# Reordering the Fourier steps, layer-norm work and one buffer switch of a hand-ordered stage in an encoder kernel

## The chip, the cores and the metric

The kernel runs on one core of one Trainium2 chip. The metric is device time in microseconds (us) of one execution. Engine names are those of the profile: PE is TensorE's matmuls and PEld its weight loads, DVE is VectorE, ACT ScalarE, POOL GpSimd, SP SyncE, which here only issues DMAs.

## The reference

Two sequences (2048 and 4096 tokens, 1024 channels, fp32) pass through one encoder layer:

```
h = rms_norm(x, pre_g)
a_u, a_v, a_gate, b_in, b_gate, c_in, c_gate = split(h @ w_in)        # widths 384 x5, 256 x2
ya = (gelu(a_u) * (w_s @ layer_norm(gelu(a_v)) + b_s)) * silu(a_gate) # 4 heads x 96, chunks of 128 tokens
yb = (pooled_mean(b_in) - b_in) @ w_b * scale * silu(b_gate)          # windows 2, 4, 8, 16
yc = real(fft2(c_in)) @ c_w * silu(c_gate)                            # over positions and 64 channels
y  = x + rms_norm(concat(ya, yb, yc) @ w_out, post_g)
```

The three parts are called the mixing branch (ya), the pool branch (yb) and the Fourier branch (yc) here.

## The kernel before, in words

The program has three stages. The first (0 to 483.7 us of the trace) computes the norm statistics, the inputs of the Fourier branch and its gates, and v (`a_v`), and leaves all of that and the operands of the later products in DRAM. The third (from 1389.1 us) is the output projection. Neither is touched.

The second stage is ordered by hand: every engine does its instructions in the order in which the program writes them. It computes the remaining wide projections by a scheme with seven products instead of eight, P1, P2, X1, X2, X3, Y1, Y2, each from a fp32 operand of 1024 tokens that is split into a high part (a cast on ACT, L137) and a low part (a subtraction on DVE, L138); a product of split parts is three matmuls (`mm3`, L141 to L143). The list `todo` holds 84 products, called **slots** here and counted from 0: six blocks of the pool branch (slots 0 to 41, in the order P1 X1 P2 X2 Y1 X3 Y2), then six of the mixing branch (slots 42 to 83, P1 X1 P2 X2 X3 Y1 Y2). Each slot has three groups of 12 matmuls, one for each third of the 384 output channels. `slot()` writes, in this order: the loads of the operand two slots on, the stores that wait (`stores`), weight loads, the last eviction of the slot before (`tail`), the cut of the next slot's operand, group 1, `fill_a`, its eviction, a Fourier step, group 2, weight cuts, `fill_b`, its eviction, a Fourier step, group 3, and `then` (the 128x128 mixing products). P1, X1, X2 and X3 add up in the same three PSUM banks (`Ab`, tag A in the figures below: `Aa_0` to `Aa_2`); P1 is copied out by ACT before X1 of the next slot goes on in its bank.

All loads and stores are issued by SP, in order, on one queue.

**Fourier steps.** `steps` is the list of the Fourier branch's work, and each call of `beside()` advances it by one: call n issues the store of step n-4, the load of step n, the compute part of step n-2 and the `pre` part of step n. A step may be empty. The list has

- ten **folds** (`fold_steps`): VectorE differences and sums of a sequence's halves, `fo` and `fz` (L948, L950, L138), loaded from `zz_d` and stored to `o_d`. Each fold is four steps: load, a **copy step**, compute with store, empty. The seven real copy steps (`copy_step`) are three DRAM-to-DRAM copies of weights each, that the mixing block's and the output's weight loads read;
- six **table steps** between the second and the third fold, of which two compute (tables `ttab`, `cmix`);
- for both sequences and both channel pairs a **transform** (`transform_steps`): levels 4096 (the long sequence only), 2048, 1024, whose steps load a matrix `mt` (L1018) and half an `o` (L1015) and add products `pd` in a PSUM bank of the two of tag G; the level's last step (`finish`) evicts it (`ev`, L1044, `eg`, L1045) into the row `T`. Then two base steps (`base_step`: products `pbc`, `pbs`, evictions `bm` and `T`), an empty step, and mixing steps (`mix_steps`: `pmx`, and `pny` for the last position).

Fourier tiles of one shape class share seven buffers (`ftile`, L278).

**The switch of buffers.** Pool branch and mixing branch use the same SBUF space (`e1`). Slot 42 is therefore written apart (the end of the listing): its three groups of matmuls, then all pool work that is left (`means`, `sums`, `silu`, `gate`, `close_sequence`), the stores, the closing of the pool's buffers and the opening of the mixing branch's, and only then the evictions of P1 (`ua`, L1474) and two Fourier steps.

**The mixing block.** `load_v` loads v of a half block (four chunks), `stats` computes its layer-norm statistics (DVE, L1409, L1410, and POOL), `normalise` applies them (16 ACT activations `vn`, L1423), `mix` multiplies by `w_s` (PE), `mixed`, `gelu`, `silu` and `gate` do the rest. `normalise(0)` stands in `fill_a` of the third slot of a block, `normalise(1)` in `fill_a` of the fifth.

Of the kernel before, what the change touches and what calls it, by code (L numbers as in the profile page):

```python
# [10 lines left out]
F32 = mybir.dt.float32  # L11
# [4 lines left out]
P = 128  # L16
# [17 lines left out]
def hybrid_encoder(  # L34
# [849 lines left out]
    def table_steps():  # L884
# [38 lines left out]
        return [Step(), Step(), Step(compute, load), Step(compute_mix, load_mix), Step(), Step()]  # L923
# [3 lines left out]
    def fold_steps(s, L, r):  # L927
# [40 lines left out]
        return [Step(load), copies.pop(0), Step(compute, store=store), Step()]  # L968
# [12 lines left out]
    copies += [Step(), Step(), Step()]  # L981
    T_of = {}

    def transform_steps(s, pair):
        S = SEQS[s]
        out = []

        def open_t():
            T_of[(s, pair)] = fpool.tile([P, SEQS[0] // 2 + 1], F32, tag="T", name=f"T{s}_{pair}")

        L = S
        while L >= 1024:
            out.extend(level_steps(s, L, pair, open_t if L == S else None))
            L //= 2
        for which in range(2):
            out.append(base_step(s, pair, which))
        out.append(Step())
        for kb in range(S // 2 // TB):
            out.extend(mix_steps(s, pair, kb))
        return out  # L1000

    def level_steps(s, L, pair, open_t):
# [64 lines left out]
        out.append(Step(finish))  # L1067
# [88 lines left out]
    steps[8:8] = table_steps()  # L1156
# [13 lines left out]
    def slot(j, pairs, evict, fill_a=(), fill_b=(), loads=(), then=None, cuts=(), late=False):  # L1170
# [41 lines left out]
    edge = e1.tile([P, 216], F32, name="edge")  # L1212
    corr_sb = e1.tile([P, 48], F32, name="corr_sb")
# [4 lines left out]
    def pool_means(z, n, t, name, corr_at=None):  # L1218
# [3 lines left out]
        a = e1.tile([P, TB + 16], F32, tag="a", name=f"pa{name}", bufs=6)  # L1222
        b = e1.tile([P, TB + 16], F32, tag="w", name=f"pb{name}", bufs=2)
# [5 lines left out]
        else:  # L1229
# [4 lines left out]
            else:  # L1234
                c = e1.tile([P, TB + 16], F32, tag="w", name=f"pc{name}", bufs=2)
# [110 lines left out]
    for b in range(NB // 2):  # L1346
# [18 lines left out]
        for i, m in enumerate(WIDE["b"]):  # L1365
# [7 lines left out]
            slot(7 * b + i, pairs, lambda t, ps, m=m, blk=blk: blk.evict(m, t, ps), fa[i], fb[i], loads, None, cuts, 3)  # L1373
# [3 lines left out]
    class MixBlock:  # L1377
# [6 lines left out]
        def new(self, tag, h):  # L1384
            (self.u if tag == "u" else self.ga)[h] = [
                e1.tile([P, TB], F32, tag=f"{tag}{h}", name=f"{tag}a{self.b}_{h}_{t}", bufs=3) for t in range(3)
            ]

# [26 lines left out]
        def normalise(self, h):  # L1415

            st, mv, va, rv, nb = self.ln[h]
            nc.vector.scalar_tensor_tensor(nb, mv[:, :, 0], -1.0, rv, ALU.mult, ALU.mult)  # L1418
            for c in range(NCH):
# [51 lines left out]
        def evict(self, m, t, ps):  # L1471
            u, ga = self.u, self.ga
            if m == "P1":
                nc.scalar.copy(u[1][t], ps)  # L1474
            elif m == "X1":
                nc.scalar.copy(ga[0][t], ps)
            elif m == "P2":
                nc.vector.tensor_add(u[0][t], ps, u[1][t])
# [90 lines left out]
    for b in range(NB // 2):  # L1569
# [7 lines left out]
        fb = {i: [] for i in range(7)}
        fb[6].append(lambda: blk.gate(1))
        ld = {i: [] for i in range(7)}
        ct = {i: [] for i in range(7)}  # L1580
        then = {3: lambda: blk.mix(0), 5: lambda: blk.mix(1)}
        fa[2].append(lambda: blk.normalise(0))
        fa[3].append(lambda: blk.stats(1, range(2)))
        fb[3].append(lambda: blk.stats(1, range(2, 4)))
        fa[4].append(lambda: blk.normalise(1))
        if b == 0:
            ld[1].append(lambda: blk.load_v(1))
            fb[1].append(lambda: blk.stats(0, range(4)))
            ct[0].append(lambda: cut_wide_weights("X3"))
            ld[0].append(lambda: load_wide_weights("a", "Y2"))  # L1590
            ct[1].append(lambda: cut_wide_weights("Y2"))
        else:
            fa[0] += [lambda p=prev: p.silu(0)]
# [14 lines left out]
        for i, m in enumerate(WIDE["a"]):  # L1608
            ev = lambda t, ps, m=m, blk=blk: blk.evict(m, t, ps)
            j = 7 * (b + NB // 2) + i  # L1610
            if b == 0 and i == 0:
                load_operand(j + 2)
                flush(stores)
                flush(tail)
                cut_operand(j + 1)
                op = cut.pop(j)
                pss = [pr.product(m, op) for pr in pairs]
                for f in (*ld[0], *ct[0]):
                    f()
                prev.means(1, 1)  # L1620
                prev.sums(1, 2)
                prev.silu(0)
                prev.means(1, 2)
                prev.gate(0)
                prev.gate(1)
                prev.close_sequence()
                flush(stores)
                last_pool.close()
                e1 = last_pool.enter_context(tc.tile_pool(name="e1c", bufs=1, reuse_waits="tile"))
                blk.new("u", 1)  # L1630
                blk.load_v(0)
                for t, ps in enumerate(pss):
                    ev(t, ps)
                beside()
                beside()
                continue
            slot(j, pairs, ev, fa[i], fb[i], ld[i], then.get(i), ct[i])
# [261 lines left out]
```

## Time and profile before

| | us |
|---|---|
| median of 3 runs (lowest to highest) | 1869.28 (1869.02 to 1870.66) |
| the profiled execution, its own time | 1875.17 |
| its span, first to last instruction | 1873.4 |
| first stage, 0 to 483.73 | 483.73 |
| second stage, 483.73 to 1389.13 | 905.40 |
| third stage, 1389.13 to 1873.40 | 484.27 |
| PE busy over the span | 1745.1 (93%) |
| DVE, ACT, POOL busy | 1383.5 (74%), 916.6 (49%), 429.4 (23%) |

The profile comes from one execution, whose span is its first to its last instruction; the time of that execution is a little longer. The granted clock is that of TensorE as a share of its full speed; over the span it was 0.970. "Busy" leaves out issuing of DMAs, branches and semaphores. A wait is put down to the instruction that released it last.

### The profile page before, as it was taken

To read this page: it belongs to the slowest core of one execution; us is meant where nothing else is said; L and a number is where in the kernel's file an instruction comes from. 1 tells how busy PE (TensorE), PEld (TensorE's weight loads), DVE (VectorE), ACT (ScalarE), POOL (GpSimd) and SP (SyncE) were. 2 spreads that over 40 slices of the span, in tenths; PEclk is the share of its full clock that TensorE was granted. 3 is DMA by queue.
4 is the path that set the end of the run, shared out by engine and by line. 5 is a ranking of instruction groups with operands and counts; after the bars stand their busy time and mean duration, and the time that the engine had idled before them with its cause. 6 is when DMAs were issued, how large, how long until landed. Compare 5 with 4: busy or idle time off the path is not lost. (4 is left out here: it accounts for less than half of the span.)

```text
span 1873.4 us, 27630 instructions
## 1 busy us (share of the span) xinstructions
PE 1745.1 (93%) x9784; PEld 1501.4 (80%) x9784; DVE 1383.5 (74%) x2320; ACT 916.6 (49%) x1766; POOL 429.4 (23%) x293
## 2 busy tenths in 40 slices
PE   5999999999989889999698999889989999999998
PEld 4999999999867767877486877777767888888886
DVE  8867777897687896777755675556786777777786
ACT  4766653345555453456364554645663343333332
POOL 5001121321000000000000010000005656666664
PEclk9999999999999999999799999999999999999999
DMA  7999997787859978868776577564844545454543
GB/s 250 331 341 317 369 351 267 283 313 265 294 193 300 298 266 284 284 237 273 239 260 214 188 257 250 175 239 146 276 131 159 169 155 178 160 168 158 169 157 112
DMA packets 221787, 443.83 MB, mean 237 GB/s; under 512 B 30417, under 2 KB 112977, under 8 KB 221649
## 3 DMA queue, kind: packets, MB, share of 16 engines
q1 hardware_dynamic: 221648, 442.07, 68.8%
q8 instruction: 77, 1.26, 0.3%
q14 instruction: 62, 0.50, 0.1%
HBM read 297.81 MB, written 150.47 MB: 239 GB/s over the span
## 5 line engine op out<-in xcount | busy, mean ns | idle before, releaser
L1413 POOL TENSOR_TENSOR lnst<-lnst,mhalf 128x16 f32<-128x16 f32 x12 | 37.3, 3106 | 434.5 <-DVE lnst L1412 414.2
L1731 POOL TENSOR_TENSOR cc<-cc,xr 128x1024 f32<-128x1024 f32 x46 | 110.4, 2400 | 53.4 <-DVE cc L1730 53.4
L398 DVE SCALAR_TENSOR_TENSOR xp<-xp,g_sb,rbc 128x256 f32<-128x256 f32 x192 | 98.8, 580 | 4.7 <-ACT rbc L382 3.2
L1423 ACT ACTIVATE vn<-vn,lnst 128x96 f32<-128x96 f32 x192 | 70.2, 454 | 51.4 <-DVE lnst L1418 51.4
L1672 ACT ACTIVATE junk<-cc 128x512 f32<-128x512 f32 x72 | 45.5, 632 | 80.9 <-DVE cc L1713 45.1
L137 ACT CAST yo_X<-y 128x512 fp32r<-128x512 f32 x60 | 34.9, 620 | 89.3 <-PE Xo L143 74.4
L138 DVE TENSOR_TENSOR yo_P<-y,yo_P 128x512 fp32r<-128x512 f32 x48 | 70.1, 1460 | 7.1 <-ACT yo_P L137 6.9
L1268 POOL MEMSET zb<- 128x16 f32 x6 | 0.5, 112 | 322.0 <-ACT zb L1266 261.3
L365 ACT ACTIVATE xrow<-xrow 128x512 f32<-128x512 f32 x88 | 54.9, 627 | 21.6 <-DMA xrow<-in_x_sample 20.7
L1730 DVE SCALAR_TENSOR_TENSOR cc<-cc,orr,pgb 128x512 f32<-128x512 f32 x69 | 53.8, 807 | 15.3 <-POOL orr L1680 15.3
L353 POOL TENSOR_TENSOR rr<-ssq,mhalf 128x4 f32<-128x4 f32 (+1 forms) x13 | 17.0, 1311 | 201.7 <-DVE ssq L351 138.9
L138 DVE TENSOR_TENSOR yo_X<-y,yo_X 128x512 fp32r<-128x512 f32 x48 | 59.4, 1238 | 0.2
L141 PE MATMUL pd<-mt,o 128*128 128x256 f32 (+1 forms) x80 | 27.9, 349 | 24.1 <-ACT eg L1045 9.9
L1672 ACT ACTIVATE junk<-Po 128x512 f32<-128x512 f32 x24 | 14.4, 599 | 72.3 <-PE Po L143 72.3
L137 ACT CAST yo_P<-y 128x512 fp32r<-128x512 f32 x48 | 29.4, 615 | 40.1 <-PE Xo L143 26.1
L177 DVE TENSOR_TENSOR ys<-y,y 128x512 f32<-128x512 f32 x24 | 23.8, 996 | 32.7 <-DMA y<-yc_d 32.6
L1680 POOL TENSOR_TENSOR orr<-oms,mhalf 128x1 f32<-128x1 f32 x48 | 27.1, 565 | 83.4 <-DVE oms L1678 83.4
L1409 DVE BATCH_NORM_STATS2 lnst<-vn 128x6 f32<-128x96 f32 x192 | 44.2, 230 | 0.0
L141 PE MATMUL Ab<-b_X1h,wbX1h 128*128 128x512 f32 x72 | 31.1, 432 | 14.0 <-ACT zb L1331 13.7
L1239 ACT COPY pa<-pb 32x512 f32<-32x512 f32 (+1 forms) x24 | 14.8, 619 | 58.6 <-DVE pb L1227 36.5
L191 POOL TENSOR_TENSOR y<-y,y 128x512 f32<-128x512 f32 x23 | 32.8, 1428 | 31.2 <-DVE yo_X L138 27.4
L1410 DVE BATCH_NORM_AGGREGATE lnst<-lnst 128x2 f32<-128x6 f32 x192 | 35.0, 182 | 6.6
(740 smaller groups left out, 6750.2 us busy)
## 6 DMA issues: line engine op xcount, KB each, us to landing
op_d<-xp SPq DMA_DIRECT2D x72, 512.0 KB, 5.9
mt<-const_m SPq DMA_DIRECT2D x56, 512.0 KB, 6.5
xp<-in_xt SPq DMA_DIRECT2D x48, 512.0 KB, 6.4
out<-cc SPq DMA_DIRECT2D x46, 512.0 KB, 2.9
xr<-in_x_sample SPq DMA_DIRECT2D x32, 512.0 KB, 4.2
xrow<-in_x_sample SPq DMA_DIRECT2D x28, 512.0 KB, 5.8
o<-o_d SPq DMA_DIRECT2D x40, 256.0 KB, 5.5
vn_d<-vg SPq DMA_DIRECT2D x48, 192.0 KB, 4.2
```

The source lines that it names most:

```text
L137: last_cast[0] = nc.scalar.copy(hi, src)
L138: return (nc.gpsimd if pool_lo else nc.vector).tensor_sub(lo, src, hi.bitcast(F32))
L141: nc.tensor.matmul(ps, lh, rh, start=first, stop=False, skip_group_check=True)
L365: nc.scalar.activation(half, half, AF.Square, accum_out=ss[:, 2 * c + h : 2 * c + h + 1])
L398: nc.vector.scalar_tensor_tensor(xs[q][:, sl], xs[q][:, sl], g8_sb[:, 4 * kh + k : 4 * kh + k + 1], rbc[a], ALU.mult, ALU.mult,)
L1409: nc.vector.bn_stats(st[:, j], self.v[h][c][:, 96 * hd : 96 * hd + 96])
L1410: nc.vector.bn_aggr(mv[:, j], st[:, j])
L1413: nc.gpsimd.tensor_tensor(rv, va, mhalf, ALU.pow)
L1423: nc.scalar.activation(v_, v_, AF.Identity, bias=nb[:, j : j + 1], scale=rv[:, j : j + 1])
L1672: nc.scalar.activation(junk, src, AF.Square, accum_out=ss[:, j : j + 1])
L1730: nc.vector.scalar_tensor_tensor(cc[c][:, hs], src, rr, pgb[:, hs], ALU.mult, ALU.mult)
L1731: nc.gpsimd.tensor_add(cc[c], cc[c], xr[c])
```

## The change

- **Empty steps.** Behind the last step of each level, and behind each base step, stands an empty step (before: one behind the two base steps).
- **Folds and copies.** The seven copy steps and three table steps (one empty) come first in the list, one to a call; folds have an empty step in the copy step's place.
- **Three steps to a slot.** `slot()` takes `more`: further calls of `beside()` behind the third group. It is 1 in the slots X1, P2, Y1 and X3 of the pool blocks 3 to 5 and in the slots X2 and Y1 of each mixing block. The list now has 168 steps.
- **The switch.** Slot 42 is written by `slot()` like the rest. P1 of the first mixing block goes into three tiles `s1a` of the Fourier branch's seven buffers; the pool's last `means`, `sums`, `silu` and `gate` stand in `fill_a` and `fill_b`, and `change_buffers` (stores, closing, opening, then both `load_v`) in the new place `fill_c`, ahead of the third group. `close_sequence` moves to slot 44; its tiles come out of the Fourier buffers and out of `mpool`.
- **The mixing block.** `normalise` takes a range of chunks. Chunks 0 and 1 of half 0 are done in `fill_b` of the third slot and 2 and 3 in its `fill_c`; those of half 1 in `fill_b` of the fifth and `fill_a` of the sixth. `gelu(0)` moves from `fill_a` to `fill_b` of the fourth slot, the first block takes its own `u` tiles of half 1 in the fifth slot, and the tile `m` has one buffer instead of two.

```
@@ table_steps
-        return [Step(), Step(), Step(compute, load), Step(compute_mix, load_mix), Step(), Step()]
+        return [Step(compute, load), Step(compute_mix, load_mix), Step()]
@@ fold_steps
-        return [Step(load), copies.pop(0), Step(compute, store=store), Step()]
+        return [Step(load), Step(), Step(compute, store=store), Step()]
@@ copies
-    copies += [Step(), Step(), Step()]
@@ transform_steps
         for which in range(2):
-            out.append(base_step(s, pair, which))
-        out.append(Step())
+            out.extend([base_step(s, pair, which), Step()])
@@ level_steps
-        out.append(Step(finish))
+        out.extend([Step(finish), Step()])
@@ the list
-    steps[8:8] = table_steps()
+    steps[0:0] = [*copies, *table_steps()]
@@ slot
+        for f in fill_c:
+            f()
         last = pairs[2].product(m, op)
+        for _ in range(more):
+            beside()
         if then:
             then()
@@ pool_means
-        a = e1.tile([P, TB + 16], F32, tag="a", name=f"pa{name}", bufs=6)
-        b = e1.tile([P, TB + 16], F32, tag="w", name=f"pb{name}", bufs=2)
+        def tile_(x, tag, bufs):
+            if n < TB:
+                return ftile(f"p{x}{name}", (P, n + 16))
+            return e1.tile([P, TB + 16], F32, tag=tag, name=f"p{x}{name}", bufs=bufs)
+        a, b = tile_("a", "a", 6), tile_("b", "w", 2)
@@ the pool blocks
-            slot(7 * b + i, pairs, ..., cuts, 3)
+            slot(7 * b + i, pairs, ..., cuts, 3, (), 1 if b > 2 and i in (1, 2, 4, 5) else 0)
@@ MixBlock
-        def normalise(self, h):
+        def normalise(self, h, cs):
...
-            for c in range(NCH):
+            for c in cs:
...
-                m_ = e1.tile([P, NCH, P], F32, tag="m", name=f"m{self.b}_{h}_{t}", bufs=2)
+                m_ = e1.tile([P, NCH, P], F32, tag="m", name=f"m{self.b}_{h}_{t}")
...
             if m == "P1":
-                nc.scalar.copy(u[1][t], ps)
+                nc.scalar.copy(self.s1[t], ps)
@@ the mixing blocks
-            3: [lambda: blk.new("g", 1), lambda: blk.gelu(0)], 4: [lambda: blk.mixed(0)], 5: [],
+            3: [lambda: blk.new("g", 1), lambda: blk.stats(1, range(2))], 4: [lambda: blk.mixed(0)],
+            5: [lambda: blk.normalise(1, range(2, 4))], 6: [...],
...
-        fa[2].append(lambda: blk.normalise(0))
-        fa[3].append(lambda: blk.stats(1, range(2)))
-        fb[3].append(lambda: blk.stats(1, range(2, 4)))
-        fa[4].append(lambda: blk.normalise(1))
+        fb[2] += [lambda: blk.normalise(0, range(2))]
+        fc[2] += [lambda: blk.normalise(0, range(2, 4))]
+        fb[3] += [lambda: blk.gelu(0), lambda: blk.stats(1, range(2, 4))]
+        fb[4] += [lambda: blk.normalise(1, range(2))]
         if b == 0:
+            blk.s1 = [ftile(f"s1a_{t}", (P, TB)) for t in range(3)]
+            def change_buffers():
+                nonlocal e1
+                flush(stores)
+                last_pool.close()
+                e1 = last_pool.enter_context(tc.tile_pool(name="e1c", bufs=1, reuse_waits="tile"))
+                blk.load_v(0)
+                blk.load_v(1)
...
+            fa[0] += [lambda p=prev: p.means(1, 1), lambda p=prev: p.sums(1, 2), lambda p=prev: p.silu(0)]
+            fb[0] += [lambda p=prev: p.means(1, 2), lambda p=prev: p.gate(0), lambda p=prev: p.gate(1)]
+            fc[0] += [change_buffers]
+            fc[2] += [prev.close_sequence]
...
-            slot(j, pairs, ev, fa[i], fb[i], ld[i], then.get(i), ct[i])
+            slot(j, pairs, ev, fa[i], fb[i], ld[i], then.get(i), ct[i], False, fc[i], 1 if i in (3, 5) else 0)
```

The first place is ACT in slot 51, the third slot of the second mixing block, from the cast of X2's operand to that of X3's. `vn` are the 16 normalisations, `ev` and `eg` the evictions of a level of the Fourier transform. Before:

```order
L137 CAST a_X2h<-a_X2l 128x1024 x2
L1423 ACTIVATE vn_0_9567<-vn_0_9567,lnst_0_9822 128x96 x4
L1423 ACTIVATE vn_1_9569<-vn_1_9569,lnst_0_9822 128x96 x4
L1423 ACTIVATE vn_2_9571<-vn_2_9571,lnst_0_9822 128x96 x4
L1423 ACTIVATE vn_3_9573<-vn_3_9573,lnst_0_9822 128x96 x4
L1044 COPY ev_4096_1_9987<-pd_4096_10_9173 128x512
L1045 ACTIVATE eg_4096_1_9988<-pd_4096_10_9173,cols 128x512
L137 CAST a_X3h<-a_X3l 128x1024 x2
```

With the change:

```order
L137 CAST a_X2h<-a_X2l 128x1024 x2
L1042 COPY ev_2048_1_10019<-pd_2048_10_9841 128x256
L1043 ACTIVATE eg_2048_1_10020<-pd_2048_10_9841,cols 128x256
L1433 ACTIVATE vn_0_9593<-vn_0_9593,lnst_0_9865 128x96 x4
L1433 ACTIVATE vn_1_9595<-vn_1_9595,lnst_0_9865 128x96 x4
L1433 ACTIVATE vn_2_9597<-vn_2_9597,lnst_0_9865 128x96 x4
L1433 ACTIVATE vn_3_9599<-vn_3_9599,lnst_0_9865 128x96 x4
L137 CAST a_X3h<-a_X3l 128x1024 x2
```

The normalisations now stand behind the evictions of the Fourier step, which is another level's step than before, since the list has moved.

The second place is ACT in slot 42, from the last SiLU `gb` of the pool branch to the cut of the operand of slot 44. `pa_..l` are the tiles of `close_sequence`, `Aa` the PSUM banks of P1, `ua` its place before and `s1a` now. Before:

```order
L1283 ACTIVATE gb_0_2_8502<-gb_0_2_8502 128x512
L1285 COPY gb_1_2_8658<-gb_0_2_8502 128x8
L1239 COPY pa_0l<-pb_0l 32x8
L1239 COPY pa_1l<-pb_1l 64x8
L1239 COPY pa_2l<-pc_2l 32x8
L1474 COPY ua_1_0_9100<-Aa_0_8987 128x512
L1474 COPY ua_1_1_9101<-Aa_1_9000 128x512
L1474 COPY ua_1_2_9102<-Aa_2_9013 128x512
L137 CAST a_P2h<-a_P2l 128x1024 x2
```

With the change:

```order
L1290 ACTIVATE gb_0_2_8515<-gb_0_2_8515 128x512
L1292 COPY gb_1_2_8676<-gb_0_2_8515 128x8
L1484 COPY s1a_9016<-Aa_0_9031 128x512
L855 CAST waX3h<-waX3l 128x1536
L1484 COPY s1a_9017<-Aa_1_9067 128x512
L1484 COPY s1a_9018<-Aa_2_9121 128x512
L137 CAST a_P2h<-a_P2l 128x1024 x2
```

The copies of `close_sequence` are gone from here, one weight cut stands between the evictions, and these write tiles that the new pool does not hold.

The third place is SP from the last store of the pool branch (`yb_d`) on, in slots 42 to 44. `vn` are the loads of v, `a_X2l` is the operand of slot 45, `o` and `mt` belong to a Fourier step. Before:

```order
L1325 DMA yb_d_124<-pa_2l 128x8
L1395 DMA vn_0_9103<-vn_d 128x384
L1395 DMA vn_1_9105<-vn_d 128x384
L1395 DMA vn_2_9107<-vn_d 128x384
L1395 DMA vn_3_9109<-vn_d 128x384
L1130 DMA yc_d_125<-gm_0_20_8850 128x512
L1130 DMA yc_d_125<-gm_0_21_8852 128x512
L1015 DMA o_4096_10_9116<-o_d_4096_127 128x512
L1018 DMA mt_4096_100_9118<-const_m 128x1024
L1018 DMA mt_4096_101_9130<-const_m 128x1024
L826 DMA a_X2l<-op_d 128x1024 x2
```

With the change:

```order
L1319 DMA yb_d_124<-pa_1_2_9045 128x512
L1404 DMA vn_0_9105<-vn_d 128x384
L1404 DMA vn_1_9107<-vn_d 128x384
L1404 DMA vn_2_9109<-vn_d 128x384
L1404 DMA vn_3_9111<-vn_d 128x384
L1404 DMA vn_0_9113<-vn_d 128x384
L1404 DMA vn_1_9115<-vn_d 128x384
L1404 DMA vn_2_9117<-vn_d 128x384
L1404 DMA vn_3_9119<-vn_d 128x384
L826 DMA a_X2l<-op_d 128x1024 x2
L1013 DMA o_4096_13_9159<-o_d_4096_127 128x512
L1016 DMA mt_4096_130_9161<-const_m 128x1024
```

Eight loads of v instead of four stand behind the stores, and the operand and the next matrix now come behind these.

## Rows read from the trace of the kernel before

**Rows 1.** The page: span and instructions

```profile
span 1873.4 us, 27630 instructions
```

**Rows 2.** Busy time of the hand-ordered stage (us, engines' busy, PEclk, DMA share, GB/s)

```profile
483.73:1389.13 905.40, 825.81 (x4571) 674.36 (x4570) 632.39 (x1240) 469.96 (x848) 41.17 (x30) 0.95 0.71 241
```

**Rows 3.** The same, slots 9, 26, 64, 4-8, 25, 42-43, 51, 63-65, 71-72

```profile
573.43:581.59 8.16, 8.16 (x37) 6.76 (x36) 6.36 (x14) 3.73 (x5) 0.00 (x0) 1.00 0.70 229
...
738.02:747.54 9.52, 9.52 (x43) 7.88 (x42) 3.05 (x3) 5.61 (x13) 0.22 (x2) 1.00 0.71 249
...
1161.79:1170.70 8.91, 8.91 (x43) 7.47 (x42) 5.55 (x22) 4.24 (x7) 1.49 (x1) 1.00 0.85 276
...
516.37:573.43 57.06, 46.22 (x189) 36.17 (x188) 45.04 (x72) 29.97 (x60) 0.00 (x0) 0.91 0.65 214
...
721.27:738.02 16.75, 12.71 (x43) 9.60 (x42) 12.24 (x17) 5.30 (x8) 0.00 (x0) 0.80 0.80 278
...
894.21:936.20 41.99, 24.41 (x87) 19.25 (x86) 31.39 (x79) 13.86 (x24) 2.90 (x1) 0.76 0.68 229
...
1009.97:1028.25 18.28, 11.93 (x44) 9.38 (x43) 5.79 (x9) 9.38 (x21) 0.00 (x0) 0.81 0.40 144
...
1148.82:1186.51 37.69, 31.55 (x137) 25.96 (x136) 19.07 (x53) 19.75 (x39) 2.90 (x1) 0.91 0.62 202
...
1240.70:1270.41 29.71, 23.27 (x94) 18.92 (x92) 9.94 (x28) 12.64 (x27) 2.90 (x1) 0.83 0.50 180
```

**Rows 4.** PE's waits in that stage: who waited for whom, total us, times, longest

```profile
PE Ab L141 <- ACT zb L1331: 13.7, 3, 6.0
PE pny L1142 <- ACT ua L1474: 13.1, 1, 13.1
PE pd L141 <- ACT eg L1045: 9.9, 4, 5.6
PE pd L141 <- DMA mt<-const_m: 6.7, 3, 4.0
PE pbs L1088 <- ACT T L1060: 4.6, 1, 4.6
PE pd L141 <- DVE lnst L1409: 4.5, 1, 4.5
PE pbc L1088 <- ACT bm L1090: 3.9, 1, 3.9
```

**Rows 5.** DVE groups, 500 to 720 us: line, operation, xcount, busy us, mean ns

```profile
L948 DVE TENSOR_TENSOR fo<-fz,fz 128x132 f32<-128x132 f32 (+1 forms) x80 | 17.2, 284 | 4.1 <-DMA fz<-zz_d 4.0
...
L950 DVE TENSOR_TENSOR fz<-fz,fz 128x512 f32<-128x512 f32 x20 | 13.8, 689 | 0.3
L138 DVE TENSOR_TENSOR fo<-fo,fh 128x512 fp32r<-128x512 f32 x20 | 13.7, 685 | 1.8 <-ACT fh L137 1.8
```

**Rows 6.** Timeline of ACT in slot 51: start, duration, line, operation

```profile
1014.23 5.84 ACT L1423 ACTIVATE vn<-vn,lnst 128x96 f32<-128x96 f32 x16 [1.57 <-DVE lnst L1418]
1019.97 0.56 ACT L1044 COPY ev<-pd 128x512 f32<-128x512 f32 x1
```

**Rows 7.** Timelines of DVE, SP and ACT in slot 42

```profile
908.55 3.86 DVE L1305 TENSOR_TENSOR pa<-pa,gb 128x512 f32<-128x512 f32 x6
...
909.26 3.49 SPq L1312 DMA_DIRECT2D yb_d<-pa  x6
...
909.91 0.20 ACT L1285 COPY gb<-gb 128x8 f32<-128x8 f32 x1
...
916.40 1.56 ACT L1474 COPY ua<-Aa 128x512 f32<-128x512 f32 x3 [0.82 <-DVE pa_2l L1323]
```

**Rows 8.** DMA issues: KB of each, median us from issue to landing

```profile
mt<-const_m SPq DMA_DIRECT2D x56, 512.0 KB, 6.5
...
yb_d<-pa SPq DMA_DIRECT2D x30, 256.0 KB, 6.4
```

**Rows 9.** Busy time of the stretch in which the transfers were densest

```profile
600.00:620.00 20.00, 20.00 (x89) 16.39 (x88) 17.93 (x31) 12.63 (x27) 0.00 (x0) 1.00 1.00 328
```

More of the change, by code (lines that the diff above doesn't have):

```diff
@@ L1168, in flush, with slot @@
             f()
-    def slot(j, pairs, evict, fill_a=(), fill_b=(), loads=(), then=None, cuts=(), late=False):
+    def slot(j, pairs, evict, fill_a=(), fill_b=(), loads=(), then=None, cuts=(), late=False, fill_c=(), more=0):
         m = todo[j][2]
@@ L1372, in hybrid_encoder @@
                     cuts.append(lambda i=i: cut_wide_weights(WIDE["b"][i - 2]))
-            slot(7 * b + i, pairs, lambda t, ps, m=m, blk=blk: blk.evict(m, t, ps), fa[i], fb[i], loads, None, cuts, 3)
+            slot(7 * b + i, pairs, lambda t, ps, m=m, blk=blk: blk.evict(m, t, ps), fa[i], fb[i], loads, None, cuts, 3, (), 1 if b > 2 and i in (1, 2, 4, 5) else 0)
         before = blk
@@ L1384, in new @@
         def new(self, tag, h):
-            (self.u if tag == "u" else self.ga)[h] = [
+            (self.u if tag == "u" else self.ga)[h] = ts_ = [
                 e1.tile([P, TB], F32, tag=f"{tag}{h}", name=f"{tag}a{self.b}_{h}_{t}", bufs=3) for t in range(3)
             ]
+            if tag == "u" and h == 1 and self.b > 0:
+                self.s1 = ts_
         def load_v(self, h):
@@ L1413, in stats @@
                 nc.gpsimd.tensor_tensor(rv, va, mhalf, ALU.pow)
[L1415 removed]
+        def normalise(self, h, cs):
             st, mv, va, rv, nb = self.ln[h]
[L1418 to L1419 removed]
+            if cs[0] == 0:
+                nc.vector.scalar_tensor_tensor(nb, mv[:, :, 0], -1.0, rv, ALU.mult, ALU.mult)
+            for c in cs:
                 for hd in range(4):
@@ L1477, in evict @@
             elif m == "P2":
-                nc.vector.tensor_add(u[0][t], ps, u[1][t])
+                nc.vector.tensor_add(u[0][t], ps, self.s1[t])
             elif m == "X2":
@@ L1572, in hybrid_encoder @@
         fa = {
-            0: [lambda: blk.new("u", 1)], 1: [lambda: blk.new("g", 0)], 2: [lambda: blk.new("u", 0)],
-            3: [lambda: blk.new("g", 1), lambda: blk.gelu(0)], 4: [lambda: blk.mixed(0)], 5: [],
-            6: [lambda: blk.silu(1), lambda: blk.mixed(1)],
-        }
[L1577 to L1580, printed above, removed]
+            0: [], 1: [lambda: blk.new("g", 0)], 2: [lambda: blk.new("u", 0)],
@@ new lines, in hybrid_encoder @@
+            3: [lambda: blk.new("g", 1), lambda: blk.stats(1, range(2))], 4: [lambda: blk.mixed(0)],
+            5: [lambda: blk.normalise(1, range(2, 4))], 6: [lambda: blk.silu(1), lambda: blk.mixed(1)],
+        }
+        fb, fc, ld, ct = ({i: [] for i in range(7)} for _ in range(4))
+        fb[2] += [lambda: blk.normalise(0, range(2))]
+        fc[2] += [lambda: blk.normalise(0, range(2, 4))]
+        fb[3] += [lambda: blk.gelu(0), lambda: blk.stats(1, range(2, 4))]
+        fb[4] += [lambda: blk.normalise(1, range(2))]
@@ L1592, in hybrid_encoder @@
         else:
-            fa[0] += [lambda p=prev: p.silu(0)]
+            fa[0] += [lambda p=prev: p.silu(0), lambda: blk.new("u", 1)]
             fb[0] += [lambda p=prev: p.gate(0), lambda: blk.stats(0, range(2))]
@@ L1610, in hybrid_encoder @@
             j = 7 * (b + NB // 2) + i
[L1611 to L1636, printed above, removed]
-            slot(j, pairs, ev, fa[i], fb[i], ld[i], then.get(i), ct[i])
+            slot(j, pairs, ev, fa[i], fb[i], ld[i], then.get(i), ct[i], False, fc[i], 1 if i in (3, 5) else 0)
         prev = blk
```

17 lines of the change are left out of this document (9 added, 8 removed).

## Prediction

> **What bounds the kernel now.** I read the page first. Its span is 1873.4 us [rows 1]. The change touches only the hand-ordered stage, 905.40 of those microseconds; PE is busy for 825.81 there and the mean granted clock is 0.95 [rows 2]. So the loss is in holes on PE, and in time after some holes at the lower of its two levels (1.2 instead of 2.4 GHz). The third view cuts that stage into slots [rows 3]. An undisturbed slot of 36 products lasts 8.16 us, one with two 512-column Fourier steps 9.52, one with a 256-column step 8.91. Whatever a slot lasts beyond that is loss: 57.06 against 5 x 8.16 = 40.8 in slots 4 to 8 (16.3 lost), 41.99 against 19.0 in slots 42 and 43 (23.0), 18.28 against 8.9 in slot 51 (9.4), 37.69 against about 27.8 in slots 63 to 65 (9.9), 29.71 against about 18.8 in slots 71 and 72 (10.9). The fourth view names what ended PE's waits [rows 4]: ScalarE copies mostly, in four places. The matmuls are the same ones after the change, so only these losses can move.
>
> **Part A, fold steps and copies (slots 0 to 9).** The seven copy steps leave the folds and run alone in slots 1 to 4; the folds start ten steps later, in slots 7, 9, 11 and so on instead of 2, 4 and then 9. A fold costs VectorE 17.2/10 + 13.8/10 + 13.7/10 = 4.5 us [rows 5]. Two of them, 9 us, leave the slots in which five weight cuts also run; this backlog is what slots 4 to 8 wait for. One fold returns in slot 7, whose P1 evictions slot 8 needs; the wait of that kind was 13.7 us in three places [rows 4], so one could cost 6 with its clock. I take 3, since no fold precedes it. The 21 DRAM-to-DRAM copies keep their bytes and come where fold loads and stores were, so I cost them at nothing; if they delayed the operands, slots 3 to 5 would wait. Gain 16.3 - 3 = **13** (6 to 16). From slot 9 to 23 folds stand where they stood, and their losses stay.
>
> **Part B, the switch of buffers (slots 42 and 43).** Before, the three P1 evictions wait in ScalarE's queue for the new pool, hence for the pool branch's gating (3.86 us, done 18.2 us into the slot); the evictions start at 916.40, and PE's next step stands behind them: 13.1 us, then 4.5 more [rows 4, 7]. Now P1 goes into three Fourier buffers, so that PE goes on. But VectorE's and ScalarE's lists up to the gating are the same but for one weight cut, and the SiLUs still stand ahead of the first eviction; they ended 15.9 us into slot 42 (910.11 less 894.21 [rows 7]). VectorE has some 2 us less to do just before, so I put the first copy's end at 13; X1's first product, due at 9.5, waits 3.5. The gating ends no earlier than the 18.2 of now, so the six yb stores still leave SP at 15 to 18 us or later (3.49 us for all [rows 7]). Behind them SP now holds eight loads of v, then X2's operand, then the matrix of the step that PE reaches first in slot 44: gating done at 20, eight loads about 4.5 (some 0.5 us an issue, as the stores show), operand and o 1.5, landing 6.5 for mt [rows 8], together 32.5. PE would want it at 9.5 + 3.5 + 9.5 + 2.7 = 25.2, and waits some 7.5; issues here also wait for older transfers, so I say 8.5. For the clock after two holes I put 5: the stretch of slots 42 and 43 ran at 0.76, 10 us of 41.99 [rows 3], about half of them inside the holes themselves. After: 3.5 + 8.5 + 5 = 17. Gain 23 - 17 = **6** (-2 if the statistics on VectorE hold up slot 45 too; 18 if the matrix comes in time).
>
> **Part C, Fourier steps in the mixing blocks (slots 44 to 75).** In slot 51 ScalarE first does 16 normalisations, 5.84 us, and only then the eviction `ev` that frees the accumulator for the next level [rows 6]; PE waits 5.6 of the 9.9 us of that kind [rows 4]. Now those 16 stand behind the second and third product, after the step's own work, and an empty step separates a level's eviction from the next level's first product, and one base step from the next. The waits on `eg`, on `T` and on `bm` (9.9 + 4.6 + 3.9 [rows 4]) are of that sort. Slots 51, 63 to 65, 71 and 72 lose 9.4 + 9.9 + 10.9 = 30.2; of this I leave 3.5 to a matrix that landed late. To it come some 6 us in single waits elsewhere (the rest of `eg`, the ny steps). Gain 26.7 + 6 = **33** (20, if one wait in three returns in another place, to 40). The vector work per slot does not grow, and the single `m` buffer costs nothing, since one engine writes and reads it.
>
> **Part D, three steps to a slot.** From slot 22 on four of seven pool slots carry three steps. A matrix buffer is freed one step before the load is issued and wanted three steps later: 1.5 slots before, now one slot of about 10.2 us less the step itself, against a landing of 6.5 [rows 8]. That holds with 2 to 3 us to spare. Traffic in such a slot is 2 x 512 KB of operand, 3 x 512 KB of matrix, 1.5 x 256 KB of o and some stores, 3.2 MB in 10.2 us or 318 GB/s; the densest stretch of the trace shows 328 GB/s at a DMA share of 1.00 [rows 9]. So transfers will run close to full, and the first step of the transform, which stands behind ten fold stores on SP, still waits. I take **-6** for waits on matrices and tables, late vector work (P1 to X1 at the start of blocks) and their clock, between -1 (none of weight) and -14 (two waits of 4 us with clock).
>
> The Trainium skill, "DMA: Bandwidth & Descriptors", section Specifications, puts the limit of HBM for one core at about 358 GB/s. By that figure a three-step slot would leave a tenth of the bandwidth free, part D would be about -2 and the time 1819. The trace does not bear it out: its share is full at 328 GB/s, so I keep -6.
>
> **Sum.** 13 + 6 + 33 - 6 = 46 us. The profiled execution took 1875.17 us, 1.8 more than its span and 5.9 more than the median of the three runs, so it would become 1829; against the median 1869.28 - 46 = **1823**. The ends are 6 - 2 + 20 - 14 = 10 and 16 + 18 + 40 - 1 = 73, that is 1859 and 1796.
>
> **Rivals.** (1) Slower: DMA cannot feed three steps to a slot. Ten three-step slots follow the start of the transform up to slot 41. If the matrix is late in each by what the first one is late now (4.0 us at the longest [rows 4]) and the clock falls each time (3.4 us, 0.20 of slot 25's 16.75 [rows 3]), 74 us go against the 52 of the other parts: 1891. It decides from about eight late slots. For it: 318 against 328 GB/s, one queue in order. Against: a late load delays the loads behind it no further, and level 4096 covers only six of these slots. (2) SP's queue at the switch is worse than I say: v loads, operand and matrix come after both the stores' landing (6.4 [rows 8]) and VectorE's statistics, and slots 44 to 47 wait in turn. Part B then loses 12, as much as the longest wait now [rows 4], in place of the 6: 13 - 12 + 33 - 6 = 28, 1841. For it: eight loads where four stood. Against: PE needs the late X2 operand only a slot later. (3) The normalisation merely moves: now behind the second product, it delays the evictions and the mixing products of its block; half of slot 51's 9.4 us in each of six blocks takes 28 from part C: 18, 1851. For it: same 5.84 us on the same engine. Against: the mixing comes a whole slot later.
>
> **How the numbers follow.** My case has 0.67, rival 2 0.15, rival 3 0.08, rival 1 0.07; 0.03 is left for no effect that can be told (0.2%, 3.7 us, is about what a measurement of this kernel can tell). The first three are faster: 0.90. The range that holds 8 in 10 takes my case from its best end over rivals 2 and 3: 1797 to 1856.
>
> **What would show it.** Right: PE's waits on `eg`, `T` and `bm` under 5 us together (18.4 now); no 13 us wait in slot 42, but one on `mt` of about 8 in slot 44; slots 4 to 8 under 46 us; the stages before and after unchanged within 2 us. Wrong: waits on `mt` over 25 us in the stage (part D), slots 4 to 8 still above 52 (part A), or the mixing products waiting for `vn` (part C).

## The result, and the profile after

The changed kernel takes 1845.58 us (median of 4 runs, 1842.88 to 1847.28); the kernel before, run again beside it, 1869.6. The ratio is 0.987, 95% interval 0.9852 to 0.9887: 24 us faster. Forecast were 1823 and a gain of 46. The range, 1797 to 1856, holds the time; the gain is half of the forecast.

The page's span and the same view by stretches as [rows 2, 3]. The stretches are the hand-ordered stage; slots 4 to 8; 22 to 25; 26 to 41; 42 and 43; 44; 46 to 75:

```profile
span 1842.9 us, 27653 instructions
...
481.09:1359.57 878.48, 815.57 (x4571) 666.98 (x4570) 631.94 (x1239) 470.61 (x847) 39.95 (x30) 0.97 0.74 248
513.73:563.83 50.10, 43.99 (x189) 35.19 (x188) 44.45 (x72) 27.40 (x57) 0.00 (x0) 0.93 0.65 208
685.21:736.36 51.15, 39.90 (x148) 31.53 (x148) 40.22 (x67) 22.09 (x39) 0.22 (x2) 0.83 0.83 268
736.36:908.12 171.76, 160.54 (x706) 131.19 (x705) 113.86 (x163) 78.88 (x140) 0.95 (x10) 0.97 0.75 262
908.12:929.10 20.98, 19.33 (x85) 15.69 (x84) 16.58 (x22) 12.30 (x19) 0.00 (x0) 1.00 0.70 249
929.10:950.82 21.72, 12.54 (x43) 9.72 (x42) 12.97 (x52) 9.11 (x22) 4.41 (x7) 0.76 0.83 293
963.87:1283.20 319.33, 310.38 (x2173) 257.68 (x2169) 214.16 (x500) 184.84 (x339) 25.19 (x9) 0.99 0.67 228
```

The kernel before in slots 22 to 25, 26 to 41 and 46 to 75:

```profile
693.84:738.02 44.18, 40.13 (x150) 32.03 (x151) 33.95 (x52) 16.55 (x26) 0.00 (x0) 0.85 0.78 262
738.02:894.21 156.19, 152.25 (x689) 125.18 (x688) 112.41 (x159) 82.22 (x150) 3.90 (x18) 1.00 0.77 264
958.09:1308.72 350.63, 324.44 (x2188) 266.72 (x2184) 214.26 (x501) 184.62 (x339) 25.48 (x9) 0.96 0.63 213
```

Fourier steps change slots, so lengths alone mislead. I call **loss** what a slot lasts beyond its own matmuls at the pace of undisturbed slots, from their PE records: 0.227 us for one of 512 columns (8.16/36), 0.120 for one of 256, 0.11 in a base step, 0.030 for one of the mixing's 128 (11.01 less 8.16, by 96, in slot 80). Summed over slots, in us:

| slots | before | after | gain | forecast |
|---|---|---|---|---|
| 0 to 8 | 16.1 | 9.1 | 7.0 | 13 (A) |
| 9 to 21 | 14.2 | 15.1 | -0.9 | 0 |
| 22 to 41 | 15.8 | 35.3 | -19.5 | -6 (D) |
| 42 to 45 | 22.6 | 14.1 | 8.5 | 6 (B) |
| 46 to 75 | 42.9 | 15.1 | 27.8 | 33 (C) |
| 76 to 83 | 9.1 | 5.1 | 4.0 | 0 |
| sum | 120.7 | 93.8 | 26.9 | 46 |

The gain by slots is more than the 24 us of the medians, because before was profiled in an execution 5.6 us above its median (1875.17) and after in one 0.9 below (1844.67). The spans differ by 30.5; the untouched stages account for 3.6 of that (481.09 against 483.73, 483.33 against 484.27) and the slots for 26.9. Every kernel below was profiled once too, in an execution up to 6.7 us off its median, so that a difference of a few us between the losses of two runs is not a difference of their times.

PE's waits in the stage (columns as in [rows 4], which they answer to):

```profile
PE pd L141 <- DMA mt<-const_m: 18.5, 5, 9.2
PE Ab L141 <- ACT zb L1338: 16.5, 4, 5.8
PE pny L1140 <- DVE gm L1122: 4.9, 1, 4.9
PE pmx L141 <- DVE gm L1122: 4.3, 3, 2.6
PE Ab L141 <- ACT b_X2h L137: 4.1, 1, 4.1
...
PE pm L1442 <- ACT vn L1433: 1.7, 1, 1.7
...
PE Aa L141 <- ACT s1a L1484: 1.6, 1, 1.6
```

No wait on `eg`, `T` or `bm` is left, but waits on the matrix have grown from 6.7 to 18.5. Three of the places in which slots lose more than was forecast follow. In slots 22 to 24 (timelines of SP and DVE: start, duration):

```profile
695.77 1.91 SPq L939 DMA_DIRECT2D fz<-zz_d  x4
...
699.62 0.30 DVE L948 TENSOR_TENSOR fo<-fz,fz 128x132 f32<-128x132 f32 x1 [5.47 <-DMA fz<-zz_d]
702.12 1.50 DVE L948 TENSOR_TENSOR fo<-fz,fz 128x132 f32<-128x132 f32 x7 [2.20 <-DMA fz<-zz_d]
...
708.17 2.35 DVE L138 TENSOR_TENSOR b_X2l<-b_X2l,b_X2h 128x1024 fp32r<-128x1024 f32 x2
```

With three steps in slot 22, a fold is computed by the third step in the slot in which it is loaded. Its loads leave SP at 695.77 us, behind the stores of the fold before; VectorE stands 7.7 us for them, and the cut of slot 24's operand (`b_X2l`) stands behind. In slots 42 and 43, SP's timeline:

```profile
923.86 3.36 SPq L1319 DMA_DIRECT2D yb_d<-pa  x6
927.32 4.62 SPq L1404 DMA_DIRECT2D vn<-vn_d  x8
932.04 0.85 SPq L826 DMA_DIRECT2D a_X2l<-op_d  x2
...
933.68 1.01 SPq L1016 DMA_DIRECT2D mt<-const_m  x2
```

This is the queue that part B described: stores, eight loads, operand, matrix, and PE waits 9.2 us for it in slot 44. In slot 66, one of three steps (timelines of DVE and PE):

```profile
1176.45 0.25 DVE L1418 BATCH_NORM_STATS2 lnst<-vn 128x6 f32<-128x96 f32 x1
...
1179.36 0.67 DVE L1122 TENSOR_TENSOR gm<-gm,pmx 128x512 f32<-128x512 f32 x1
...
1180.17 0.56 PE L1140 MATMUL pny<-cny,cmf 128*128 128x1 f32 x2 [4.93 <-DVE gm L1122]
```

`pny` needs the bank that `gm` empties, and `gm` stands behind eight of the statistics. These in turn stand behind the cut of the next operand, which waits 5.0 us for its cast on ScalarE; with the normalisation back in its old places (e10) that wait is not there and `pny` waits 2.9 instead of 4.9.

### The profile page after: what moved, and what is told of

Read it like the earlier page. It is cut to its first block, busy times and chain, and to the rows that moved or that the text cites. A ratio compares the mean times of both kernels' runs of the same rounds, so it can differ in the third digit from the quotient of the medians.

```text
span 1842.9 us, 27653 instructions
## 1 busy us (share of the span) xinstructions
PE 1735.1 (94%) x9784; PEld 1492.9 (81%) x9784; DVE 1381.5 (75%) x2320; ACT 916.9 (50%) x1766; POOL 430.6 (23%) x293
## 5 line engine op out<-in xcount | busy, mean ns | idle before, releaser
L398 DVE SCALAR_TENSOR_TENSOR xp<-xp,g_sb,rbc 128x256 f32<-128x256 f32 x192 | 93.0, 550 | 5.1 <-ACT rbc L382 3.8
L141 PE MATMUL pd<-mt,o 128*128 128x256 f32 (+1 forms) x80 | 27.2, 340 | 20.3 <-DMA mt<-const_m 18.5
```

The costliest lines, as they stand in the source:

```text
L141: nc.tensor.matmul(ps, lh, rh, start=first, stop=False, skip_group_check=True)
L398: nc.vector.scalar_tensor_tensor(xs[q][:, sl], xs[q][:, sl], g8_sb[:, 4 * kh + k : 4 * kh + k + 1], rbc[a], ALU.mult, ALU.mult,)
```

## The experiments

Theory at the start: each part acts in its own slots, as in the table. Twelve kernels followed, each timed beside the kernel before.

| run | median, us | ratio to before (95%) |
|---|---|---|
| e1 third steps in block 5 alone | 1857.04 | 0.9923 (0.9899 to 0.9947) |
| e2 none in slots 22, 23 | 1835.34 | 0.981 (0.9773 to 0.9847) |
| e3 none in the mixing blocks | 1855.91 | 0.9934 (0.9914 to 0.9955) |
| e4 matrix first at the switch | 1844.04 | 0.9865 (0.9829 to 0.9901) |
| e5 before, empty steps alone | 1872.85 | 1.0016 (1.0004 to 1.0029) |
| e6 before, switch alone | 1867.97 | 0.9989 (0.9971 to 1.0006) |
| e7 before, normalisation alone | 1845.93 | 0.9872 (0.985 to 0.9895) |
| e8 before, copies alone | 1886.32 | 1.0089 (1.0062 to 1.0115) |
| e9 e2 and the switch mended | 1837.82 | 0.9825 (0.9799 to 0.985) |
| e10 change, normalisation undone | 1842.64 | 0.9856 (0.9825 to 0.9888) |
| e11 before, normalisation and switch | 1843.07 | 0.9858 (0.9818 to 0.9898) |
| e12 e9, statistics later | 1833.72 | 0.9805 (0.9779 to 0.9831) |

### What the third steps cost (e1, e2, e3)

e1:

```
-... 1 if b > 2 and i in (1, 2, 4, 5) else 0)
+... 1 if b > 4 and i in (1, 2, 4, 5) else 0)
```

> The changed kernel with third steps in the last pool block alone (slots 36, 37, 39, 40): eight of the twelve third steps of the pool blocks are gone. Theory (third steps cost the pool slots): slots 22 to 35 lose about 15 us beyond their own work, as before the change, where they lose 33 with it; the list ends four slots later, which costs up to 3; time 1830 to 1836. Rival (the twenty microseconds more that slots 22 to 41 lose come from the later start and the empty steps, not from the third steps): loss in slots 22 to 41 stays near 41, time 1843 to 1848.

Slots 22 to 41 lose 13.5 instead of 35.3, as the theory has it. The time is 11 us worse all the same: the list stands elsewhere at the switch, and slots 42 to 45 lose 43.3 instead of 14.1. PE's longest wait there, and then ScalarE's wait behind it:

```profile
PE pmx L141 <- ACT th L137: 18.0, 1, 18.0
```

```profile
ACT th L137 <- DMA yc_d<-gm: 22.5, 1, 22.5
```

Mixing steps meet the switch now. `th` (the high part of a mixing step's input) waits for a buffer whose last store (`yc_d<-gm`) is itself late on SP. That `s1a` holds three of the seven buffers then makes this likelier; it was not tried without them.

e2:

```
-... 1 if b > 2 and i in (1, 2, 4, 5) else 0)
+... 1 if 7 * b + i > 23 and i in (1, 2, 4, 5) else 0)
```

> The changed kernel without the third step in slots 22 and 23 alone. Theory (in slot 22 the third step computes a fold in the slot in which it is loaded, so VectorE stands 7.7 us for fz and the operand cuts behind it come late): slots 23 and 24 take 8.2 us each instead of 12.4 and 12.0, the wait for a matrix in slot 25 stays at 4 to 6; time 1836 to 1839. Rival (transfers are full there, so the wait only moves): slot 25 or 26 takes the 8 us over, time 1843 to 1847.

The time falls to 1835. Busy time in slots 22 to 25 and in slot 26:

```profile
687.23:721.58 34.35, 34.35 (x145) 28.29 (x145) 27.57 (x43) 15.74 (x25) 0.00 (x0) 0.95 0.87 290
721.58:744.01 22.43, 11.48 (x43) 9.05 (x42) 13.16 (x25) 7.83 (x17) 0.22 (x2) 0.77 0.68 233
```

Slots 23 and 24 take 8.16 us each, so the fold computed in the slot of its load was the cause. The matrix's wait, expected to stay at 4 to 6, moved from slot 25 to 26 and grew to 11.0, because on SP it stands behind the last fold's stores, which wait 10.6 us for that fold on VectorE and ScalarE (SP's waits from 700 to 740 us, then its timeline):

```profile
SPq L961 <- ACT fh L137: 11.0, 2, 10.6
```

```profile
733.29 0.45 SPq L1016 DMA_DIRECT2D mt<-const_m  x1
```

So slots 22 to 41 lose 24.5, 10.8 less than with the change: about what the time shows.

e3:

```
-            slot(..., fc[i], 1 if i in (3, 5) else 0)
+            slot(..., fc[i], 0)
```

> The changed kernel without third steps in the mixing blocks; those of the pool blocks stay. Theory (the third step's products wait for the PSUM bank of the step just before, whose emptying stands behind the statistics on VectorE): slots 66 and 73 lose about 2.5 us each beyond their work instead of 10.0 and 4.7, the list ends later, in slots 76 to 80, which costs up to 4; time 1835 to 1842. Rival (third steps are what kept the levels off the evictions): new waits of 2 to 5 us on eg, bm or T in three or more slots, time 1846 to 1852.

Slots 66 and 73 are clean, as the theory has it, but the time rises to 1856: the list ends late, and slots 76 to 83 lose 17.8 instead of 5.1 (expected at most 4 more). Neither reading foresaw where; PE's longest waits from slot 76 on:

```profile
PE pny L1140 <- DVE gm L1122: 4.2, 1, 4.2
PE Ya L141 <- DVE m L1455: 4.1, 1, 4.1
```

Slots 46 to 75 lose only 2.4 us less, since other waits come up there. The third steps of the mixing blocks cost little and save 13 us by ending the list early.

### Each part alone on the kernel before (e5 to e8)

e5:

```
-            out.append(base_step(s, pair, which))
-        out.append(Step())
+            out.extend([base_step(s, pair, which), Step()])
-        out.append(Step(finish))
+        out.extend([Step(finish), Step()])
```

> The kernel before with one thing of the change: an empty step behind each level's last step and behind each base step. Theory (the gain of the mixing blocks comes from keeping a level's eviction and the next level's first product apart): the waits on eg, T and bm (18.4 us) fall below 6, but the list ends seven slots later, in slots 81 and 82, where late steps cost up to 13; time 1852 to 1866. Rival (the empty steps do nothing without the moved normalisation, which is what the evictions stand behind): waits on eg, T and bm stay above 12; time 1868 to 1878.

From 955 to 1290 us, about slots 46 to 75, PE's waits on ScalarE's `eg`, `T` and `bm` fall from 17.4 to 3.2, and the loss of these slots from 42.9 to 30.2; waits of 8.5 us of `pny` on `gm` stand there instead of 1.8. At the switch a mixing step meets the late P1 copies, and slots 42 to 45 lose 30.2 instead of 22.6 (PE's waits):

```profile
PE Aa L141 <- ACT ua L1473: 15.5, 1, 15.5
PE pny L1141 <- ACT vn L1422: 7.8, 1, 7.8
```

By the medians it is 3 us slower than before: the mechanism works, but the time does not show it. The switch takes 7.6 of the 12.7 back; the rest is less than the 8 us by which the two profiled executions differ from their medians.

e6 has the diff's switch (`s1a`, `change_buffers`, `tile_`, the slot's `fill_c`, the new places of the last pool work and of `close_sequence`) and its single buffer of `m`, and nothing else of it.

> The kernel before with the change's switch of buffers alone (P1 in Fourier buffers, the new place of the stores, loads and close_sequence). Theory: slots 42 and 43 lose 3 us instead of 23, slot 44 loses 12 more to a matrix that is issued behind the stores and eight loads of v; net gain 6 to 10, time 1859 to 1864. Rival (other Fourier steps fall on the switch here than in the changed kernel, and what they wait for decides): a gain below 3 or a loss, time 1866 to 1880.

No difference that can be told. Slots 42 to 45 lose 18.2 instead of 22.6: the matrix is late here too (6.5), and `pny` in slot 42 waits 5.7 for `gm`. The truth lies between the two readings.

e7:

```
-        fa[2].append(lambda: blk.normalise(0))
-        fa[4].append(lambda: blk.normalise(1))
+        fb[2].append(lambda: blk.normalise(0, range(2)))
+        fc[2].append(lambda: blk.normalise(0, range(2, 4)))
+        fb[4].append(lambda: blk.normalise(1, range(2)))
+        fa[5].append(lambda: blk.normalise(1, range(2, 4)))
```

(and `gelu(0)` from `fa[3]` to `fb[3]`.)

> The kernel before with the normalisation in two parts and in the change's places, gelu with it. Theory: slot 51 loses 2 us instead of 9.4, the waits of 2 to 4 us on eg, bm and T in slots 54, 63, 65 and 72 shrink by half; time 1856 to 1862. Rival (the sixteen activations only stand in front of something else, the late evictions or the mixing products): time 1866 to 1872.

**As much as the whole change, from this part alone**: 1845.93 against 1845.58, and more than expected. Slots 46 to 75 lose 17.0 instead of 42.9. ScalarE's timeline in slot 51, as in [rows 6], then the two largest of PE's waits left from 955 to 1290 us:

```profile
1014.33 0.59 ACT L1044 COPY ev<-pd 128x512 f32<-128x512 f32 x1
...
1018.51 5.85 ACT L1426 ACTIVATE vn<-vn,lnst 128x96 f32<-128x96 f32 x16 [3.00 <-DVE lnst L1421]
```

```profile
PE pny L1142 <- DVE gm L1124: 5.8, 2, 3.2
PE pd L141 <- ACT eg L1045: 2.2, 1, 2.2
```

The eviction is done before the 16 activations begin.

e8: the diff of `table_steps`, `fold_steps`, `copies` and the list.

> The kernel before with the copies and table steps ahead of the folds. Theory (five weight cuts and two folds no longer share VectorE): slots 0 to 8 gain 7 us; the transforms start two slots later, which moves their waits without adding to them; time 1860 to 1865. Rival (what stands two slots later meets other work, as in the run with third steps in the last pool block alone): the gain of 7 is lost in slots 42 to 83; time 1867 to 1876.

17 us slower. The 7 us are there (slots 0 to 8 lose 9.5 instead of 16.1), and slots 22 to 25 lose 7 less than before, but the transforms start two slots later and meet other work. PE's waits from slot 46 on:

```profile
PE pd L141 <- ACT eg L1044: 12.4, 2, 7.2
PE pbs L1087 <- ACT T L1059: 6.3, 1, 6.3
PE pbc L1087 <- ACT bm L1089: 5.5, 1, 5.5
```

Slots 26 to 41 lose 21.4 instead of 5.6 (waits of 4.8 for `eg`, 3.8 for the cut of `b_Y2l` and 2.1 for `T` among them), slots 42 to 45 some 4 more than before, and slots 46 to 75 lose 47.8 instead of 42.9. This is the rival, and worse than it said.

### Is the normalisation needed? (e10)

```
-        fb[2] += [lambda: blk.normalise(0, range(2))]
-        fc[2] += [lambda: blk.normalise(0, range(2, 4))]
-        fb[4] += [lambda: blk.normalise(1, range(2))]
+        fa[2] += [lambda: blk.normalise(0, range(4))]
+        fa[4] += [lambda: blk.normalise(1, range(4))]
```

(and `gelu(0)` and the second half of `normalise(1)` back.)

> The changed kernel with the normalisation and gelu back in the places of before; all else of the change stays. Theory (the moved normalisation carries the whole gain, the rest of the change comes to about nothing): time 1864 to 1874, with waits on eg, T or bm behind the 16 activations. Rival (the empty steps of the change keep the evictions away from the normalisations, so that either of the two is enough): time 1845 to 1855.

The theory that e7 suggested falls: without the moved normalisation the change is as fast as with it. ScalarE's timeline in slots 51 and 52, then PE's only wait over 2 us from 955 to 1290 us:

```profile
1016.37 5.85 ACT L1433 ACTIVATE vn<-vn,lnst 128x96 f32<-128x96 f32 x16 [1.56 <-DVE lnst L1428]
1022.12 0.35 ACT L1042 COPY ev<-pd 128x256 f32<-128x256 f32 x1
```

```profile
PE pny L1140 <- DVE gm L1122: 2.9, 1, 2.9
```

The eviction again stands behind the 16 activations, and nobody waits for it: an empty step lies between it and the next level's first product, the part that took most of these waits away in e5 too. Slots 46 to 75 lose 13.1. The moved normalisation alone (e7) or the rest of the change alone (e10) takes the same 26 to 30 us there; the other adds nothing. Of the rest, e5 shows the empty steps to part evictions and products; what the third steps add to that was not tried alone.

### Mending what is left (e4, e9, e11, e12)

e4:

```
             part(i - 2, "store")
-            part(i + 2, "load")
+            if i + 2 not in early:
+                part(i + 2, "load")
@@ change_buffers
                 nonlocal e1
+                early.append(at[0] + 2)
+                part(at[0] + 2, "load")
                 flush(stores)
...
-                blk.load_v(1)
+            fc[1] += [lambda: blk.load_v(1)]
```

> The changed kernel with the next Fourier step's matrix loaded ahead of the pool's last stores, and the second load of v moved behind slot 43's steps. Theory (the matrix of slot 44 is late because SP issues it only after six stores, eight loads of v and an operand): the wait of 9.2 us falls to 0 to 3 and the lower clock behind it (5.1) goes with it; time 1831 to 1836. Rival (the landing is slow because the transfers of that stretch share the engines, whatever the order of issue): the wait stays above 6, time 1842 to 1846.

Slot 44's wait falls to 2.3 and its loss from 12.2 to 2.7, as the theory has it, but the time does not move: slot 45 now waits 6.8 for the next matrix. SP's timeline:

```profile
943.15 0.79 SPq L826 DMA_DIRECT2D a_Y1l<-op_d  x2
950.57 0.32 SPq L1333 DMA_DIRECT2D yb_d<-pa_0l  x1
...
954.49 0.96 SPq L1017 DMA_DIRECT2D mt<-const_m  x2
```

SP stands 7 us for stores of `close_sequence`, whose copies ScalarE does behind 16 normalisations. That wait lay hidden behind the first.

e9 is e2 with e4's edit and

```
-            fc[2] += [prev.close_sequence]
+            fb[2].insert(0, prev.close_sequence)
```

> The changed kernel without third steps in slots 22 and 23, with the next matrix ahead of the pool's last stores, the second load of v behind slot 43's steps, and close_sequence ahead of the normalisations of slot 44 on ScalarE. Theory (in the run with the matrix first, the wait of slot 45 came from three stores of 128x8 in SP's queue, which wait for ScalarE's copies behind 16 normalisations): slot 44 loses about 3 and slot 45 about 3, where the run without third steps over the folds lost 12 and 3; time 1824 to 1829. Rival (the switch holds SP for so long that the next matrix is late whatever stands first): one of slots 44 to 47 loses 8 or more, time 1833 to 1838.

The time is in the rival's range and slot 45 loses about 8, but not whatever stands first in the queue: now the third of the small tiles is late, since it needs one of the seven Fourier buffers and waits for PE to finish with one (timelines of DVE and SP):

```profile
940.32 0.18 DVE L1244 TENSOR_TENSOR pc_2l<-pb_2l 128x17 f32<-128x17 f32 x1 [3.98 <-PE pd L143]
...
941.51 0.32 SPq L1333 DMA_DIRECT2D yb_d<-pa_2l  x1
...
942.34 0.91 SPq L1017 DMA_DIRECT2D mt<-const_m  x2
```

e11 is e7, e6 and the mended switch on the kernel before.

> The kernel before with the moved normalisation and the mended switch; no empty steps, no third steps, copies where they were. Theory (parts that act in different slots add up): slots 46 to 75 lose about 40 as with the normalisation alone, slots 42 to 45 lose 10 instead of 26.5; time 1828 to 1833. Rival (the step that stands at the switch here waits for something else, as the switch alone showed with 5.7 us in slot 42): slots 42 to 45 lose over 18, time 1837 to 1845.

Slots 42 to 45 lose 15.5, between the two readings; the time is within the interval of e7's, so the switch again adds nothing that can be told.

e12 is e9 with

```
-            3: [..., lambda: blk.stats(1, range(2))]
-        fb[3] += [lambda: blk.gelu(0), lambda: blk.stats(1, range(2, 4))]
+        fb[3] += [lambda: blk.gelu(0), lambda: blk.stats(1, range(2))]
+        fc[3] += [lambda: blk.stats(1, range(2, 4))]
```

> As the run with the mended switch and no third steps over the folds, and besides the statistics of the second half one place later in the fourth slot of each mixing block (behind the second and ahead of the third group). Theory (the wait of pny or pmx for gm in the three-step slots comes from 8 statistics that stand ahead of gm on VectorE): the slot with that wait (59 there) loses about 3 instead of 9.5, time 4 to 7 us below that run. Rival (the wait comes from the operand's cut, which the second half of the normalisation delays on ScalarE): the wait stays above 3 us, time within 2 us of that run.

4 us below e9 (the two intervals overlap), and slots 46 to 75 lose 9.8 instead of 19.2. Slot 59 takes 14.42 us instead of 21.98, at the full clock, and its wait of `pny` for `gm` falls from 5.6 to 0.7, as the theory has it; slot 67 gives 4 back, where a product now waits 3.3 us for `gny`. Slot 59 in e9 and the same stretch in e12:

```profile
1088.09:1110.07 21.98, 16.33 (x148) 13.34 (x146) 11.86 (x42) 13.89 (x28) 2.90 (x1) 0.84 0.73 248
```

```profile
1093.00:1107.50 14.50, 13.83 (x148) 11.35 (x147) 10.03 (x40) 11.88 (x22) 0.11 (x1) 1.00 0.94 333
```

e2, e9 and e12 are faster than the change (their intervals end at 0.9847, 0.985 and 0.9831, below its 0.9852), and e12 and e2 by these runs not apart from each other: mending the switch and the statistics on top of e2 brought nothing that can be told. The largest loss left in e12 is slot 26, where the matrix waits 10.4 us; it was not tried to start the transforms a slot later.

## Why the prediction was right, and where not

The direction, the range and the bound (holes on PE) were right, and so was the mechanism of the largest term, C. That the time fell inside the range is in part luck: the steps below that came out worse than forecast cost some 25 us together, D alone more than its own worst case, and 6.5 came back from B and from slots that were not in the sum. Of the signs that the prediction named, the waits on `eg`, `T` and `bm` (none left) and the wait for a matrix in slot 44 (9.2) came as said; slots 4 to 8 took 50.10, neither under 46 nor above 52, and the first stage ran 2.6 us shorter, though nothing in it was touched. Rival 1 would have shown over 25 us of waits on `mt` (18.5 came), rival 3 mixing products that wait for `vn` (one did, 1.7). By its own steps:

- **Part A, 13, was 7.0.** Slots 4 to 8 went from 57.06 to 50.10. The backlog of folds and weight cuts was the cause. Mis-sized was the step "I take 3, since no fold precedes it": the returning fold in slot 7 costs 6.8 (a wait of 4.5 and lower clock in slots 7 and 8, [rows 4] had up to 6.0 for one), and 1.9 stays in slot 6. As an edit alone it costs 17 us (e8), because it moves everything behind it; that was not in the sum at all.
- **Part B, 6, was 8.5.** The first copy holds PE for 1.65 us (3.5 said) and the matrix comes 9.2 late (8.5 said). What slot 44 loses beyond that wait, 12.2 less 9.2, is 3.0 at a mean granted clock of 0.76; the forecast had 5 for the clock. Rival 2 did not occur.
- **Part C, 33, was 27.8 in slots 46 to 75.** The waits on `eg`, `T` and `bm` are gone. Not foreseen were slots 66 and 73 (7.8 and 2.5), where third steps wait behind the statistics. The two reasons given for C, normalisation behind the evictions and empty steps, were counted as one effect, which they are: either side gives it without the other (e7, e10), while the empty steps by themselves end the waits on `eg`, `T` and `bm` but take only 12.7 of the loss (e5).
- **Part D, -6 and at worst -14, was -19.5. This is the step that failed.** It weighed transfers, 318 against 328 GB/s, and the landing of a matrix. 8.1 of it is slots 23 and 24, a fold computed in the slot of its load (e2), with no lack of transfer rate: slots 22 to 25 ran at 268 GB/s and a share of 0.83. The rest is in single waits of 1.7 to 2.6 us and the time behind them, in slots 29, 32, 36 and 39: for a matrix, for `pa` and `gm` on VectorE, for a table. They too came with the third steps (with none before slot 36, in e1, slots 22 to 41 lose 13.5), but why each was late was not followed further. That two of the three-step slots lay over folds stood in the list and was not looked at.
- **Slots 76 to 83** gained 4.0 that were not forecast. Before, slot 77 waits 2.0 us for a store of the mixing branch (`Aa` for `ya_d<-ua`) and slots 77 and 78 lose 3.9 in all; after, they lose 0.6. Why that store is no longer late was not looked into.

The page "DMA: Bandwidth & Descriptors" of the Trainium skill, section Specifications, would by its 358 GB/s have made D -2, an estimate. What e2 takes out of D is the order of the work, which neither estimate holds. The ground on which the prediction set the page's figure aside does not stand either: [rows 9] are not the densest stretch of that trace, and its share is not full at 328 GB/s. Other stretches of 20 us in the kernel before, one in the hand-ordered stage and one in the first, moved more than the page's limit:

```profile
714.00:734.00 20.00, 15.96 (x58) 12.32 (x57) 17.88 (x25) 7.82 (x11) 0.00 (x0) 0.83 1.03 364
...
200.00:220.00 20.00, 20.00 (x149) 20.00 (x148) 12.00 (x21) 10.90 (x26) 7.00 (x5) 1.00 1.01 388
```

By these rows 318 GB/s left more room than part D and rival 1 allowed for.

The sum's form failed too. Alone, the parts come to about -24 (normalisation), +17 (copies), +3 (empty steps) and -2 (switch, not told from none), -6 in all; the third steps, which were not tried alone, are missing from this. Together they give -24, and all but the normalisation -27 (-33 to -21, e10). Waits that sit between two lists, the steps' and the slots', depend on which step meets which slot.

## What to carry to other kernels

Where a list of steps runs beside a hand-ordered loop, any step added or taken away moves every later meeting of the two; count the losses by slot, and redo the whole list of who meets whom, before adding up parts. Two edits that keep the same producer and consumer apart are one gain, not two: undo each in the full version before crediting it. When steps are packed denser, look first at the shortest distance from a step's load to its compute part on each in-order queue, and only then at bandwidth.

## What the runs showed of the hardware

At the switch PE waited 1.65 us in slots 42 and 43 and kept a granted clock of 1.00; behind the wait of 9.2 us in slot 44 the mean of that slot was 0.76. Transfers took 388 GB/s over 20 us of the first stage with PE busy throughout, and 333 at a share of 0.94 in slot 59 of e12, with PE busy for 13.83 of 14.50 us. At a share of about 1 the rate was 328 in one stretch [rows 9] and 364 or 388 in others, so the share alone does not tell the rate that is left.
